# A feed-forward output by seven block products instead of eight, in three passes

## The chip, the cores and the metric

The kernel runs on one core of a Trainium2 chip. Its engines work beside each other, each through its own list of instructions in order: PE multiplies matrices into PSUM, DVE and ACT do elementwise work, POOL helps now and then, and SP issues most of the DMAs. The metric is the device time of one execution in microseconds (us), the median of several runs.

## The reference

One denoising step of a two-layer network on 512 latent and 128 prompt tokens, model width 1024, everything in fp32. Layer 0 mixes latent attention and neighbourhood attention, layer 1 is grouped-query attention. Every sub-layer is modulated by (shift, scale, gate), which come from two conditions (latent and prompt) through `w_mod`; each layer ends in a SwiGLU feed-forward of width D_FF = 2816 = 22 blocks of 128:

```python
hp = modulate(rms_norm(xp, norm_ffn[l]), sh2_p, sc2_p)
hs = modulate(rms_norm(xs, norm_ffn[l]), sh2_s, sc2_s)
xp = xp + g2_p * swiglu(hp, w_ffn_in[l], w_ffn_out[l])
xs = xs + g2_s * swiglu(hs, w_ffn_in[l], w_ffn_out[l])
...
def swiglu(h, w_in, w_out):
    gate, up = jnp.split(h @ w_in, 2, axis=-1)
    return (jax.nn.silu(gate) * up) @ w_out
```

Outputs are the normed token streams and the caches' new rows.

## The kernel before

Activations stand feature-major: a tile is 128 features by T = 640 tokens, worked on in two halves of HT = 320 columns (half 0 is latent; half 1 is 192 latent and 128 prompt columns, which is why a gated residual on it takes two instructions). Every fp32 product is three fp32r matmuls, high x high, high x low and low x high (`mm3`, L181): each operand is split by an ACT copy (the high part) and a DVE subtraction (the low part).

Layer 1's attention ends in an output projection (`mixer_out`, L1036, name "oc"): eight columns of 24 matmuls per half, a residual and a sum of squares for each, then the norm of half 0 and, later, of half 1. From the normed activations `ModS` makes the operands of the feed-forward ("h11...") with their sums and differences.

The feed-forward's input (`ffn`, L1126) does three hidden blocks directly and 19 by seven products instead of eight (Strassen's method as Winograd arranged it, on a 2 x 2 arrangement of gate/up by inner halves and of token halves). The seven products are named by their activation operand: a, D, N, b, c, C, E here, `11`, `"D"`, `"N"`, `21`, `22`, `"C"`, `"E"` in the code. Their weight operands wX, wY, wZ, wW are made per block from two raw 128 x 1024 tiles (L1210 to 1228). `close` (L1197) does a block's last product E after the next block's a and D, then silu, multiplication and `hidden` (L1152), which splits the block (640 columns at once) and writes its two halves to DRAM ("sp") through SP; the last three blocks stay.

The output (L1252 to 1350) needs all 22 hidden blocks for each of the eight output columns. It runs in two passes, over 9 and over 13 blocks, since PSUM and SBUF don't hold all; the blocks are read back from DRAM ("hr", `again`) into the ring of activation tiles and a pool "hd".

The gate of the feed-forward, G2, needs its own products of `w_mod` with the conditions: eight tiles of 512 KB ("wm"), on each of which DVE makes two multiply-and-sum passes of 128 x 1024 ("junk", L1364) against 1 MB of broadcast conditions ("cb"). `mod_side` (L1354) spreads them by a plan over the feed-forward's blocks (call at L1632). Layer 0's attention output has a similar helper beside it already (`beside`).

The order on each engine is set when the kernel is built, by a scheduler that walks the program with costs of its own; buffers of tile pools ("w", "ws", "u", "raw", with their counts) limit how far weights are prepared ahead.

Of the kernel before, what the change touches and what calls it, by code (L numbers as in the profile page):

```python
# [11 lines left out]
F32 = mybir.dt.float32  # L12
# [33 lines left out]
FO_ORDER = list(range(FB - 3, FB)) + list(range(FB - 3))  # L46


@with_exitstack
def body(ctx, tc, xT, vecs, crow, wm0, wm0g1, wm0g, wm1, wA, wNV, wNA, wMK, wMV, wOA, wGQ, wGK, wGV, wOC,  # L50
         wFI, wFO, cckvT, ckrT, cnkT, cnv, cgkT, cgv, rpbp, tabM, tabK, tabG, maskN,
# [199 lines left out]
    class ModS:  # L251


        def __init__(self, name, x, gsl, ml, sh, pools):
            pool, keep_ = pools

            a = keep_.tile([P, 2 * D], F32, tag="cb", bufs=1, name=name + "32a")
            d = [pool.tile([P, 1024], F32, tag="wr", bufs=2, name=f"{name}32d{i}") for i in range(2)]
            room = [t[:, j * HT:j * HT + HT] for t, n in ((a, 6), (d[0], 3), (d[1], 3)) for j in range(n)]
            room += [tp.tile([P, HT], F32, tag="u", bufs=7, name=f"{name}32u{i}") for i in range(4)]  # L260
            self.left, self.right = room[:KT], room[KT:]
# [774 lines left out]
    def mixer_out(wsrc, os_, order, xin, ml, name, nxt, pre, beside=None):  # L1036
# [5 lines left out]
        if True:  # L1042
# [13 lines left out]
            held = []  # L1056
            for n in range(KT):
                un = wunit(n)
                if beside and n >= 1:
                    beside(n - 1)  # L1060
# [49 lines left out]

    def ffn_open(l):
# [4 lines left out]
        hd = [[fk.tile([P, T], F32R, name=f"hd{l}_{i}{c}") for c in "hl"] for i in range(1)]  # L1116
        fs = ExitStack()
        fp = fs.enter_context(tc.tile_pool(name=f"fp{l}", bufs=1, reuse_waits="tile"))
# [5 lines left out]
        return ph, fk, dr, hd, fs, fp, w, pre  # L1124

    def ffn(l, x, pend, hm, nxt, side, opened):  # L1126
        ph, fk, dr, hd, fs, fp, w0, _ = opened
        turn = [0]

        def split(src, name):  # L1130

            turn[0] += 1
            t = (wp, fp)[turn[0] % 2].tile([P, 2, 1024], F32R, tag="w", bufs=3, name=name)
            S.activation(t[:, 0, :], src, AF.Copy)  # L1134
            V.tensor_tensor(t[:, 1, :], src, f(t[:, 0, :]), ALU.subtract)  # L1135
            return t[:, 0, :], t[:, 1, :]
# [13 lines left out]
        kept, spilt = {}, {}  # L1150

        def hidden(fb, sg):  # L1152

# [39 lines left out]
        hd += [[ring.tile([P, T], F32R, tag="hl", name=f"hd{l}_{i}{c}") for c in "hl"] for i in (1, 2)]  # L1193
# [14 lines left out]
        for fb in range(few, FB):  # L1208

            ru = load(wFI[l, fb, 1], 1024, f"wu{l}_{fb}r")  # L1210
            if fb == few:
                rg = load(wFI[l, fb, 0], 1024, f"wg{l}_{fb}r")
            else:
                rg = fp.tile([P, 1024], F32, tag="wr", bufs=2, name=f"wg{l}_{fb}r")
                nc.sync.dma_start(rg, wFI[l, fb, 0])
            wX = split(ru, f"wX{l}_{fb}")
            t = fp.tile([P, 2, 512], F32R, tag="w4", bufs=2, name=f"wW{l}_{fb}")
            wW = t[:, 0, :], t[:, 1, :]
            S.activation(wW[0], rg[:, 512:], AF.Copy)
            V.tensor_tensor(wW[1], rg[:, 512:], f(wW[0]), ALU.subtract)  # L1220
            s13 = fp.tile([P, 1024], F32, tag="ws", bufs=2, name=f"s13{l}_{fb}")
            V.tensor_tensor(s13[:, :512], rg[:, :512], rg[:, 512:], ALU.add)
            V.tensor_tensor(s13[:, 512:], ru[:, :512], rg[:, :512], ALU.add)
            wY = split(s13, f"wY{l}_{fb}")
            s24 = fp.tile([P, 1024], F32, tag="ws", bufs=2, name=f"s24{l}_{fb}")
            V.tensor_tensor(s24[:, :512], s13[:, 512:], rg[:, 512:], ALU.add)
            V.tensor_tensor(s24[:, 512:], s24[:, :512], ru[:, 512:], ALU.add)
            wZ = split(s24, f"wZ{l}_{fb}")
# [19 lines left out]
            job = fb, g, wW, up, sg  # L1248
        close(job)
# [541 lines left out]
```

## Time and profile before

| | us |
|---|---|
| median of 3 runs | 1519.8 |
| lowest and highest | 1515.85 and 1520.42 |
| the profiled execution's span | 1519.7 |

The span of the profiled execution is its time from first to last instruction; nothing of it is set apart, and its clock was 0.994 of full speed. In views by stage a row is a stretch of the span in us; in views by group a row is a line and engine, the operation, its tiles and shapes with the count, then busy time in us and the mean of one in ns, then idle time ahead of it and what ended it. In the chain of waits a row is a start, a duration, and what ran.

### The profile page before, as it was taken

What the parts mean: (1) busy time and instruction counts of PE and PEld (TensorE: products, weight loads), DVE (VectorE), ACT (ScalarE), POOL (GpSimd) and SP (SyncE); (2) the same over time, 40 slices, a digit from 0 to 9 for tenths busy, and PEclk for the clock granted to TensorE, in tenths of its full rate; (3) what the DMA queues carried; (4) which work ended last, traced back from release to release, by engine and by line L of the source; (5) the groups of instructions that cost most, each with busy time, mean ns of one, the idle gap of its engine ahead of it and who ended that gap; (6) DMA issues with size and microseconds to landing.
All of it is one profiled execution on the core that took longest, in us unless ns stands there. A gap on an engine that the chain in (4) does not pass through costs nothing. (4 is left out here: it accounts for less than half of the span.)

```text
span 1519.7 us, 25536 instructions
## 1 busy us (share of the span) xinstructions
PE 1467.1 (97%) x9894; PEld 1412.3 (93%) x9894; DVE 1134.0 (75%) x2150; ACT 737.9 (49%) x1426; POOL 176.7 (12%) x270
## 2 busy tenths in 40 slices
PE   5999999899999999999999999999999999999997
PEld 4989878889999999999999999989999999999997
DVE  5877788877878888946998888865988888833333
ACT  5446667753745555531223566653745555531221
POOL 0046636320000000000000122210000000000000
PEclk9999999999999999999999999999999999999999
DMA  9543341034164454568764200103154555466211
GB/s 373 197 150 119 119 136 43 15 111 153 46 219 145 163 166 162 182 210 321 234 228 133 91 29 29 56 15 97 47 205 154 170 167 167 133 245 232 86 42 70
DMA packets 73553, 215.08 MB, mean 142 GB/s; under 512 B 8152, under 2 KB 13048, under 8 KB 73048
## 3 DMA queue, kind: packets, MB, share of 16 engines
q1 hardware_dynamic: 71072, 209.04, 40.6%
q10 hardware_dynamic: 1944, 3.48, 0.7%
q8 instruction: 77, 1.26, 0.3%
q0 software_dynamic: 416, 0.93, 0.2%
q14 instruction: 44, 0.36, 0.1%
HBM read 184.96 MB, written 28.47 MB: 140 GB/s over the span
## 5 line engine op out<-in xcount | busy, mean ns | idle before, releaser
L1364 DVE SCALAR_TENSOR_TENSOR junk<-wm,cb 128x1024 bf16<-128x1024 f32 x104 | 126.8, 1220 | 3.6 <-DMA wm<-in_wm 2.9
L62 PE MATMUL gq<-h10h,wgq 128*128 128x320 f32 x256 | 65.8, 316 | 0.0
L246 POOL TENSOR_SCALAR h10h<-h10t,gs,mods 128x320 fp32r<-128x320 f32 x4 | 3.2, 792 | 439.1 <-DVE h10t L240 436.8
L1134 ACT ACTIVATE wY<-s 128x1024 fp32r<-128x1024 f32 x37 | 39.2, 1061 | 28.0 <-PE fg L62 22.5
L1134 ACT ACTIVATE wZ<-s 128x1024 fp32r<-128x1024 f32 x37 | 39.2, 1059 | 22.7 <-PE fd L62 20.7
L1135 DVE TENSOR_TENSOR wZ<-s,wZ 128x1024 fp32r<-128x1024 f32 x37 | 45.3, 1224 | 3.7 <-ACT wZ L1134 0.4
L1203 DVE TENSOR_TENSOR sg<-up,sg 128x640 f32<-128x640 f32 x37 | 30.4, 822 | 20.9 <-ACT sg L1202 20.7
L62 PEld LDWEIGHTS gq<-h10h,wgq 128*128 128x128 f32 x256 | 44.9, 189 | 0.6
L1135 DVE TENSOR_TENSOR wY<-s,wY 128x1024 fp32r<-128x1024 f32 x37 | 45.1, 1220 | 0.1
L62 PE MATMUL fg<-h01q,wgu 128*128 128x320 f32 x192 | 40.3, 316 | 0.9 <-ACT h01q L288 0.5
L1202 ACT ACTIVATE sg<-fg 128x320 f32<-128x320 f32 x37 | 16.2, 439 | 48.9 <-PE fg L62 48.9
L62 PE MATMUL gq<-h10l,wgq 128*128 128x320 f32 x128 | 39.5, 308 | 0.0
L1567 ACT ACTIVATE gp<-gs,gb,rq 128x640 f32<-128x640 f32 (+1 forms) x40 | 31.8, 795 | 15.3 <-DVE gb L1566 13.6
L314 DVE SCALAR_TENSOR_TENSOR xr<-fo,mods,xr 128x320 f32<-128x320 f32 (+2 forms) x48 | 19.6, 436 | 25.4 <-PE fo L62 25.3
L62 PE MATMUL fg<-h11N,wZ 128*128 128x320 f32 x228 | 36.6, 309 | 1.7 <-ACT p L1234 1.7
L1236 ACT ACTIVATE p<-fd 128x320 f32<-128x320 f32 x37 | 16.2, 438 | 45.2 <-PE fd L62 45.2
L62 PE MATMUL fg<-h11q,wX 128*128 128x320 f32 x228 | 36.7, 309 | 0.0
L62 PE MATMUL fg<-h11E,wW 128*128 128x320 f32 x228 | 36.6, 309 | 0.0
L62 PE MATMUL fd<-h11q,wZ 128*128 128x320 f32 x228 | 36.6, 309 | 0.0
L62 PE MATMUL fu<-h11q,wX 128*128 128x320 f32 x228 | 36.5, 309 | 0.0
L62 PE MATMUL fd<-h11D,wY 128*128 128x320 f32 x228 | 36.4, 308 | 0.0
L62 PE MATMUL fg<-h11C,wY 128*128 128x320 f32 x228 | 36.4, 308 | 0.0
(3055 smaller groups left out, 5299.1 us busy)
## 6 DMA issues: line engine op xcount, KB each, us to landing
wm<-in_wm SPq DMA_DIRECT2D x48, 512.0 KB, 4.3
mraw<-in_wm SPq DMA_DIRECT2D x8, 1024.0 KB, 13.1
mraw<-in_wm SPq DMA_DIRECT2D x16, 512.0 KB, 3.7
wmv<-in_wm0g SPq DMA_DIRECT2D x8, 512.0 KB, 3.6
wm<-in_wm0g SPq DMA_DIRECT2D x8, 512.0 KB, 5.3
x<-in_xT SPq DMA_DIRECT2D x8, 320.0 KB, 5.3
xr<-in_xT SPq DMA_DIRECT2D x8, 320.0 KB, 6.2
cb<-crs SPq DMA_DIRECT2D x2, 1024.0 KB, 7.8
```

What stands on the lines that cost most here:

```text
L62: cls.last = nc.tensor.matmul(*a, **k)
L246: G.tensor_scalar(h[:, c0:c1], t, self.gsl[:, k, 0:1], self.ml[:, self.sh + k, 0:1], ALU.mult, ALU.add)
L314: V.scalar_tensor_tensor(xo[:, c0:c1], ps[:, c0 - o:c1 - o], ml[:, g + n, c:c + 1], xi[:, c0:c1], ALU.mult, ALU.add)
L1134: S.activation(t[:, 0, :], src, AF.Copy)
L1135: V.tensor_tensor(t[:, 1, :], src, f(t[:, 0, :]), ALU.subtract)
L1202: last = S.activation(sg[:, 0:HT], g[:, :HT], AF.Silu, scale=-1.0)
L1203: V.tensor_tensor(sg, up, sg, ALU.mult)
L1236: S.activation(p5, b5[:, :HT], AF.Copy)
L1364: V.scalar_tensor_tensor(junk, raw, 1.0, cb[:, c, :], ALU.mult, ALU.mult, accum_out=mods[l][:, j0 + i, c:c + 1])
L1567: S.activation(dst, src, AF.Exp, bias=nb, scale=rq[:, j:j + 1], accum_out=ll[:, j:j + 1])
```

## The change

Layer 1's output product is done by the same seven-product scheme. The 22 hidden blocks are put in 11 pairs; a pair (inner halves) by two token halves is the 2 x 2 activation side, outputs n and n + 4 by the pair's blocks the weight side. `ffn_out_seven` runs three passes (`PASSES`): three pairs, then four, then four. A pass has four `Block`s (n = 0 to 3), each with seven products over the pass's pairs, three matmuls a pair: p1 uses a, p5 D, p6 N, p2 b, p3 c, p7 C, p4 E. p4 of a block stands after the next block's p1 and p5. Results go into the residual stream with the gate or, for the n + 4 outputs, the negated gate `ng`.

The operands' sums (D, N, C, E) are made in the input stage, in `hidden_pair`: after an even block two operands of 320 columns, after an odd one five, each by an ACT copy and a DVE subtraction, with four sums a pair. Nine pairs are spilled, seven tiles each (63 of 320 KB, where there were 38); pairs 9 and 10 stay. Pass 0 reads pair 8 back, the other passes 28 tiles each.

The weight preparation moves into a shared helper `seven`; layer 1's raw input weights use one "wr" buffer instead of two, and every other gate tile comes through the common raw buffers. Layer 1's G2 modulation (8 tiles, 16 passes of DVE, the conditions' load) moves from the feed-forward to the attention's output projection, by the numbers (2, 1, 1, 2, 1, 1, 0) of tiles at each column, and `early` has the column's own weights asked for first. The output weights are laid out anew (`wFO1`). Layer 0 keeps its method.

```diff
+PASSES = ((9, 8, 10), (0, 1, 2, 3), (4, 5, 6, 7))
+FO_PAIRS = [2 * p + i for ps in PASSES for i in range(2) for p in ps]
...
-    def mixer_out(wsrc, os_, order, xin, ml, name, nxt, pre, beside=None):
+    def mixer_out(wsrc, os_, order, xin, ml, name, nxt, pre, beside=None, early=False):
...
+                    if early:
+                        un(0)
...
+    def ffn_out_seven(x, nxt, opened, ops, spilt, split, close, last):
+
+        ph, fk, dr, hd, fs, fp, *_ = opened
+        ng = gs[0][0]
+        V.tensor_scalar_mul(ng, mods[1][:, G2:G2 + 8, :], -1.0)
...
+        def product(ps, wt, w0, pairs, what, first):
+            for k, p in enumerate(pairs):
+                a, b = [w[:, w0 + k * P:w0 + k * P + P] for w in wt]
+                t = ops[p, what]
+                mm3(ps[:, :HT], a, b, t[:, 0:HT], t[:, HT:T], first and k == 0, k == len(pairs) - 1, skip_group_check=not first)
...
+        def result(n, c, src, sign, end):
+
+            o = HALF[c][0]
+            for c0, c1, i in HCOND[c]:
+                V.scalar_tensor_tensor(x[n][:, c0:c1], src[:, c0 - o:c1 - o],
+                                       ng[:, n, i:i + 1] if sign < 0 else mods[1][:, G2 + n, i:i + 1], x[n][:, c0:c1], ALU.mult, ALU.add)
+            if end:
+                nrm.add(x[n], c)
...
+            def p1(self):
+                self.g = bank(f"fg{self.name}")
+                self.go(self.g, self.wX, 0, "a", True)
+                self.copy("p1", self.g)
+
+            def p5(self, kind="m", copied=True):
+                self.b5 = bank(f"fd{self.name}", kind)
+                self.go(self.b5, self.wY, 0, "D", True)
+                if copied:
+                    self.copy("p5", self.b5)
+
+            def p6(self):
+                self.go(self.g, self.wZ, 0, "N", False)
+                self.copy("u2", self.g)
+
+            def p2(self):
+                b2 = bank(f"fu{self.name}", "y")
+                self.go(b2, self.wX, 1, "b", True)
+                result(self.n, 0, self.add("p1", b2), 1, self.end)
+
+            def p3(self):
+                self.go(self.b5, self.wZ, 1, "c", False)
+                result(self.n, 1, self.add("u2", self.b5), 1, self.end)
+
+            def p7(self, ready=True):
+                self.go(self.g, self.wY, 1, "C", False)
+                if ready:
+                    result(self.n + 4, 1, self.add("p5", self.g), -1, self.end)
+                else:
+                    self.copy("u3", self.g)
+
+            def p4(self):
+                self.go(self.g, self.wW, 0, "E", False)
+                result(self.n + 4, 0, self.g, -1, self.end)
...
+        def again(p, what, pool, tag, bufs):
+            t = ops[p, what] = pool.tile([P, T], F32R, tag=tag, name=f"or{p}{what}", **({"bufs": bufs} if bufs else {}))
+            nc.sync.dma_start(f(t), spilt[p, what])
+
+        for what in PRODUCTS:
+            again(8, what, ring, "hh" if what in "aDNbc" else "hl", None)
+        b0 = Block(0, 0, 0)
+        b0.p1()
+        close()
...
+        for i, pairs in enumerate(PASSES):
+            if i:
+                for what in PRODUCTS:
+                    for p in pairs:
+                        if what in "aDNb":
+                            again(p, what, fo, "hd", 16)
+                        else:
+                            again(p, what, ring, "hl" if what == "E" else "hh", None)
...
+                if prev:
+                    prev.p4()
+                b.p6()
+                b.p2()
+                b.p3()
+                b.p7()
+                prev = b
...
+        e0, e1 = ends
+        e0.p1()
+        e0.p2()
+        prev.p4()
+        e1.p1()
+        e0.p6()
+        e1.p2()
+        e0.p7(False)
+        e1.p6()
+        e0.p4()
+        e1.p7(False)
+        e1.p4()
+        for b in ends:
+            b.p5(copied=False)
+            result(b.n + 4, 1, b.add("u3", b.b5), -1, True)
+            result(b.n, 1, b.held["u2"], 1, False)
+            if b is e0:
+                nrm.rstd(0)
+        for b in ends:
+            b.go(b.b5, b.wZ, 1, "c", False)
...
+        def operand_of(p, what, src):
+            t = ops[p, what] = pair_tile(p, what)
+            S.activation(t[:, 0:HT], src, AF.Copy)
+            V.tensor_tensor(t[:, HT:T], src, f(t[:, 0:HT]), ALU.subtract)
+            if p not in RESIDENT:
+                d = spilt[p, what] = dr.tile([P, T], F32, name=f"sp{p}{what}")
+                nc.sync.dma_start(d, f(t))
+
+        def hidden_pair(fb, sg):
+
+            p, odd = divmod(fb, 2)
+            le, ri = sg[:, 0:HT], sg[:, HT:T]
+            if not odd:
+                even[p] = sg
+                operand_of(p, "a", le)
+                V.tensor_tensor(le, le, ri, ALU.subtract)
+                operand_of(p, "D", le)
+                return
+            d, b12 = [even[p][:, c0:c1] for c0, c1 in HALF]
+            n, c = [utile(f"{q}{l}_{fb}") for q in "nc"]
+            V.scalar_tensor_tensor(n, ri, -1.0, d, ALU.mult, ALU.subtract)
+            operand_of(p, "N", n)
+            operand_of(p, "b", le)
+            operand_of(p, "c", ri)
+            V.tensor_tensor(c, ri, b12, ALU.subtract)
+            operand_of(p, "C", c)
+            V.scalar_tensor_tensor(n, n, -1.0, le, ALU.mult, ALU.subtract)
+            operand_of(p, "E", n)
...
+        if l:
+            return ffn_out_seven(x, nxt, opened, ops, spilt, split, lambda: close(job), lambda: last)
...
+    _, before = mod_side([(1, wm1[G2:], G2)], None)
+    x, pend = mixer_out(wOC, oGs, list(range(8)), lambda n, x=x: x[n], mods[1], "oc", nxt, op[-1],
+                        before(op[5], op[5], (2, 1, 1, 2, 1, 1, 0)), True)
...
-    side, _ = mod_side([(1, wm1[G2:], G2)], lambda kind, i: int(kind == "n" or i > 5 and i % 2 == 0))
-    x, pend = ffn(1, x, pend, box["m"], final, side, op)
+    x, pend = ffn(1, x, pend, box["m"], final, lambda pool: lambda kind, i: None, op)
```

On DVE, at the end of the attention's output projection ("oc" are its sums and weights, "xr" the residual stream, "wgu" the first feed-forward weights, "h11t" the first normed tile), there stood before:

```order
L172 TENSOR_TENSOR ocw_12359<-ocw7r,ocw_12359 128x1024
L206 TENSOR_TENSOR ocnacc<-ocnacc,ocnsq_12282 128x320
L314 SCALAR_TENSOR_TENSOR xr_4646<-oc5a,mods_99,xr_4646 128x320
L206 TENSOR_TENSOR ocnacc<-ocnacc,ocnsq_12317 128x320
L314 SCALAR_TENSOR_TENSOR xr_4684<-oc6a,mods_99,xr_4684 128x320
L206 TENSOR_TENSOR ocnacc<-ocnacc,ocnsq_12352 128x320
L314 SCALAR_TENSOR_TENSOR xr_4722<-oc_12355,mods_99,xr_4722 128x320
L206 TENSOR_TENSOR ocnacc<-ocnacc,ocnsq_12387 128x320
L282 TENSOR_TENSOR h11t_12461<-xr_4367,ocnrs 128x320
```

and now:

```order
L1602 SCALAR_TENSOR_TENSOR junk_12333,mods_99<-wm_46_12329,cbo 128x1024
L174 TENSOR_TENSOR ocw_12367<-ocw6r,ocw_12367 128x1024
L311 SCALAR_TENSOR_TENSOR xr_4646<-oc5a,mods_99,xr_4646 128x320
L1602 SCALAR_TENSOR_TENSOR junk_12372,mods_99<-wm_47_12370,cbo 128x1024
L208 TENSOR_TENSOR ocnacc<-ocnacc,ocnsq_12362 128x320
L1602 SCALAR_TENSOR_TENSOR junk_12374,mods_99<-wm_47_12370,cbo 128x1024
L174 TENSOR_TENSOR ocw_12409<-ocw7r,ocw_12409 128x1024
L1606 TENSOR_TENSOR mods_99<-mods_99,vec 128x16
L311 SCALAR_TENSOR_TENSOR xr_4684<-oc6a,mods_99,xr_4684 128x320
L174 TENSOR_TENSOR wgu_0_12444<-wgu_0r,wgu_0_12444 128x1024
L208 TENSOR_TENSOR ocnacc<-ocnacc,ocnsq_12404 128x320
L1176 TENSOR_SCALAR gs_100<-mods_99 128x16
```

Modulation passes ("junk") now stand between the residuals and ahead of the last weights' splits, and the feed-forward's first weights come after the last of these.

On DVE, in the input stage around odd block 13's multiplication ("sg"; "up" and "g" are sums that read PSUM, "s" weight sums, "w" splits), before:

```order
L1364 SCALAR_TENSOR_TENSOR junk_14942,mods_99<-wm_45_14940,cb 128x1024
L1226 TENSOR_TENSOR s_16_14749<-s_16_14743,wg_16r 128x512
L1364 SCALAR_TENSOR_TENSOR junk_14944,mods_99<-wm_45_14940,cb 128x1024
L1203 TENSOR_TENSOR sg_13_14357<-up_13_14356,sg_13_14357 128x640
L1220 TENSOR_TENSOR wW_15_14604<-wg_15r,wW_15_14604 128x512
L1227 TENSOR_TENSOR s_16_14749<-s_16_14749,wu_16r 128x512
L1156 TENSOR_TENSOR hd_1l<-sg_13_14357,hd_1h 128x640
L1242 TENSOR_TENSOR up_14_14492<-fu_14_14491,p_14_14494 128x320
L1135 TENSOR_TENSOR wX_16_14737<-wu_16r,wX_16_14737 128x1024
```

and now:

```order
L1451 TENSOR_TENSOR sg_13_14562<-up_13_14561,sg_13_14562 128x640
L1161 TENSOR_TENSOR wW_15_14832<-wg_15r,wW_15_14832 128x512
L1387 SCALAR_TENSOR_TENSOR n_13_14742<-sg_13_14562,sg_12_14408 128x320
L1391 TENSOR_TENSOR c_13_14743<-sg_13_14562,sg_12_14408 128x320
L1370 TENSOR_TENSOR op6N<-n_13_14742,op6N 128x320
L1370 TENSOR_TENSOR op6b<-sg_13_14562,op6b 128x320
L1370 TENSOR_TENSOR op6c<-sg_13_14562,op6c 128x320
L1370 TENSOR_TENSOR op6C<-c_13_14743,op6C 128x320
L1393 SCALAR_TENSOR_TENSOR n_13_14742<-n_13_14742,sg_13_14562 128x320
L1478 TENSOR_TENSOR up_14_14696<-fu_14_14695,p_14_14698 128x320
L1480 TENSOR_TENSOR up_14_14696<-fd_14_14694,u_14_14700 128x320
```

One split of 640 columns and a modulation pass went; three sums and five splits of 320 came, the last of them behind the next block's first two sums.

On SP, at the end of the second pass ("sp" is the spilled tile, "or" its place, "ru" and "rg" raw weights of a block), what stood from the middle of the output stage on before:

```order
L1275 DMA wo_0_60r<-in_wFO 128x640
L1275 DMA wo_0_65r<-in_wFO 128x512
L1256 DMA hr_18h<-sp_18h 128x640
L1256 DMA hr_18l<-sp_18l 128x640
L1275 DMA wo_0_75r<-in_wFO 128x512
L1275 DMA wo_1_01r<-in_wFO 128x768
L1275 DMA wo_1_11r<-in_wFO 128x768
L1275 DMA wo_0_70r<-in_wFO 128x640
```

and now, between the second and third pass:

```order
L1183 DMA rgo_1_17003<-in_wFO 128x1024
L1183 DMA ruo_2_17137<-in_wFO 128x1024
L1265 DMA or4a<-sp4a 128x640
L1265 DMA or5a<-sp5a 128x640
L1265 DMA or6a<-sp6a 128x640
L1265 DMA or7a<-sp7a 128x640
L1265 DMA or4D<-sp4D 128x640
L1265 DMA or5D<-sp5D 128x640
L1265 DMA or6D<-sp6D 128x640
L1265 DMA or7D<-sp7D 128x640
```

Reloads were spread among weight loads; now 24 of them (up to `or7C`) stand in one row behind the third block's first weights.

171 lines of the change are left out of this document (128 added, 43 removed).

## The prediction

> **What bounds the kernel now.** I read the page first, then the busy time by stage, then the chain of waits through the last feed-forward layer.
>
> ```profile
> span 1519.7 us, 25536 instructions
> PE 1467.1 (97%) x9894; PEld 1412.3 (93%) x9894; DVE 1134.0 (75%) x2150; ACT 737.9 (49%) x1426; POOL 176.7 (12%) x270
> ```
>
> ```profile
> 1026.80:1064.00 37.20, 37.20 (x254) 37.04 (x253) 19.42 (x36) 13.78 (x22) 2.41 (x1) 1.00 0.31 100
> 1200.00:1340.00 140.00, 140.00 (x957) 140.00 (x956) 118.09 (x166) 73.16 (x113) 0.00 (x0) 1.00 0.46 149
> 1356.00:1510.00 154.00, 153.00 (x1043) 152.58 (x1041) 55.20 (x97) 31.11 (x47) 0.00 (x0) 1.00 0.38 127
> ```
>
> Each row of the second fence is a stretch: its length, then busy time of PE, weight loads, DVE, ACT and POOL, the granted clock, the DMA share and GB/s. The first stretch is the output projection of layer 1's attention, the second its feed-forward input by seven products, the third its feed-forward output. In the last two PE never waits and the clock is full. In the output stage DVE is free two thirds of the time; in the input stage it has 21.9 us of 140 left.
>
> How fast PE issues is read from the chain, since a matmul's own duration overlaps its neighbours'.
>
> ```profile
> 1351.78 0.73 PE fo_0a L62 x5
> ...
> 1428.41 11.43 PE fo L62 x78
> ...
> 1509.02 0.02 issue
> ```
>
> 78 matmuls in 11.43 us are 0.1465 us each. The output stage before has 22 hidden blocks x 8 columns x 2 halves x 3 = 1056 of them: 154.7 us, which agrees with 1351.78 to 1509.02. One block of seven products (84 matmuls) takes 12.31 us, and a product over four pairs 1.76.
>
> **The gain.** After, the stage has 11 pairs x 4 blocks x 7 products x 3 = 924 matmuls. The 132 that go are worth 132 x 0.1465 = **19.3 us**, all on the path as long as PE stays the last to be waited for. Everything else in the change is work for DVE, ACT and the DMAs, costing only where it makes PE wait.
>
> **DVE in the input stage.** Durations of one, and idle time before it:
>
> ```profile
> L1135 DVE TENSOR_TENSOR wZ<-s,wZ 128x1024 fp32r<-128x1024 f32 x11 | 13.5, 1226 | 1.5
> L1364 DVE SCALAR_TENSOR_TENSOR junk<-wm,cb 128x1024 bf16<-128x1024 f32 x10 | 12.2, 1219 | 0.1
> L1203 DVE TENSOR_TENSOR sg<-up,sg 128x640 f32<-128x640 f32 x11 | 9.1, 823 | 4.4 <-ACT sg L1202 4.3
> L1242 DVE TENSOR_TENSOR up<-fu,p 128x320 f32<-128x320 f32 x12 | 5.9, 491 | 3.5 <-PE fu L62 3.5
> L1156 DVE TENSOR_TENSOR hd_1l<-sg,hd_1h 128x640 fp32r<-128x640 f32 x4 | 3.3, 824 | 0.6 <-ACT hd_1h L1155 0.6
> L1222 DVE TENSOR_TENSOR s<-wg_13r 128x512 f32<-128x512 f32 x1 | 0.7, 693 | 0.8 <-DMA wg_13r<-in_wFI 0.8
> L1281 DVE TENSOR_TENSOR wo_0a<-wo_0ar,wo_0a 128x768 fp32r<-128x768 f32 x1 | 1.0, 959 | 0.4 <-ACT wo_0a L1280 0.4
> ```
>
> ```profile
> L206 DVE TENSOR_TENSOR fn1acc<-fn1acc,fn1sq 128x320 f32<-128x320 f32 x13 | 6.4, 489 | 4.4 <-ACT fn1sq L205 4.4
> L314 DVE SCALAR_TENSOR_TENSOR xr<-fo,mods,xr 128x320 f32<-128x320 f32 x8 | 4.4, 550 | 8.0 <-PE fo L62 8.0
> L314 DVE SCALAR_TENSOR_TENSOR xr<-fo,mods,xr 128x192 f32<-128x192 f32 x8 | 3.3, 418 | 12.0 <-PE fo L62 12.0
> L314 DVE SCALAR_TENSOR_TENSOR xr<-fo,mods,xr 128x128 f32<-128x128 f32 x8 | 2.7, 342 | 0.0
> ```
>
> Before, a block has three splits of 1024 (3 x 1.226), five passes of 512 (5 x 0.69), three sums of 320 (3 x 0.49), the multiply and the split of 640 (0.82 each), and ten modulation passes are spread over the 11.4 blocks: 11.4 us by means. The stretch holds 140/12.31 = 11.4 blocks and 118.09 us busy, so 10.4 a block: consecutive operations overlap, and sums of means are to be taken times 0.91. After, without modulation and the 640 split, the common part is 9.4 by means; an even block adds three operations of 320 (two operands, one sum), an odd one eight (five operands, three sums). That is 10.9 and 13.3 by means, **9.9 and 12.1 us** in fact, 22.0 of the 24.6 that PE needs for the pair. DVE gets tight, but weight splits are made about a block ahead, so an odd block's lateness is made up in the even one. I cost it at nothing: PE's own 24.6 us cover it. ACT gains 7 x 0.44 - 2 x 0.74 = 1.6 us a pair, by these rows, on 6.4 a block (73.16 over 11.4); it has room.
>
> ```profile
> L1236 ACT ACTIVATE p<-fd 128x320 f32<-128x320 f32 x11 | 4.8, 438 | 14.5 <-PE fd L62 14.5
> L1155 ACT ACTIVATE hd_1h<-sg 128x640 fp32r<-128x640 f32 x4 | 3.0, 740 | 1.8 <-DVE sg L1203 1.8
> ```
>
> **DVE in the three passes.** One block of four pairs has the same splits (3 x 1.226 + 5 x 0.69), three sums and six gated additions (2 x 0.55, and 2 x (0.42 + 0.34 for the other 128 columns)): 11.2 by means, 10.2 us of PE's 12.31. With three pairs, splits of 768 and sums of 384, 8.8 of 9.23. In the last pass four squares' sums of 0.49 come on top: 12.0 of 12.31. So the first and last passes leave 0.4 and 0.3 us a block. If DVE also waits 1 us a block, each pass falls behind by 2 to 3 us, which the block prepared ahead should mostly take up. Bounds 0 and 5; I take **+1.0**.
>
> **The reloads.** Between the second and third pass 24 tiles of 320 KB (28 less E's four, loaded early) must come in, each into a place that the running block releases product by product.
>
> ```profile
> 1354.00:1364.00 10.00, 10.00 (x70) 10.00 (x69) 3.24 (x4) 4.16 (x5) 0.00 (x0) 1.00 1.04 400
> 1364.00:1374.00 10.00, 10.00 (x70) 10.00 (x69) 3.76 (x7) 1.48 (x2) 0.00 (x0) 1.00 1.04 395
> 1103.00:1117.50 14.50, 14.35 (x98) 14.09 (x97) 11.03 (x15) 5.42 (x8) 0.00 (x0) 1.00 0.81 286
> ```
>
> ```profile
> wo_70r<-in_wFO SPq DMA_DIRECT2D x1, 320.0 KB, 2.8
> ```
>
> The first two rows are such reloads, all engines busy: 395 GB/s, 0.83 us a tile. A lone tile lands in 2.8, 2.0 beyond that. Counting from the first matmul of the second pass's last block, its "a" tiles are free at 1.76, so tile number k lands at 1.76 + 0.83k + 2.0. PE comes to the new "a" at 12.3, D 14.1, N 17.6, b 19.3, c 21.1, and to C from 23.3 to 26.2, since the order mixes it with the next block's "a". The tightest is c's fourth tile: it lands at 20.4 and is needed at 22.4. The margin is 2.0 us. At the third row's 286 GB/s (1.15 a tile, a mixed stretch with engines only 0.81 busy) c's last would be 4.3 late and C's last another 0.8: 5.1 us. Bounds 0 and 5; the stretch is most like the first rows, so **+0.5**. The page "DMA: Bandwidth & Descriptors" of the Trainium skill, section "Where 436 GB/s comes from", says that HBM transfers are bound at about 358 GB/s per core; by that, an estimate, a tile takes 0.92 us and c's fourth lands at 22.1, 0.3 us ahead of its use, so the sum would stay but any slip of the queue would show. The two rows of 400 and 395 run above that figure, and the measurement decides.
>
> **The moved modulation.** Sixteen passes of 1.22 (and 0.08 to read each sum) go beside the attention's output projection.
>
> ```profile
> DVE xr L314 <- PE oc0a L62: 8.8, 1, 8.8
> ```
>
> ```profile
> 1052.67 3.52 PE oc6a L62 x24
> ...
> 1075.54 0.54 ACT ocnrs L213
> ...
> 1084.12 0.40 DVE h11t L282
> ...
> 1095.64 0.74 DVE hd_0l L1156
> ...
> 1103.97 6.82 DMA wg_3r<-in_wFI
> ...
> 1122.85 2.02 PE fg L62 x12
> ```
>
> DVE idles 8.8 us ahead of its first residual at 1026.8, and three passes stand there in the order. The other 13 (16.9 us) fall to 1026.8 to 1064, where DVE is now busy 19.42 of 37.2: 36.3 after, almost full, in an engine that also waits. PE has other columns' matmuls to go on with, but the first half's norm comes later, and from 1075.54 on the chain runs through ACT and DVE, so that lateness is handed on. At best 0, at worst one half column, 3.52; I take **+1.5**.
>
> **The transition to seven products.** The chain now waits 6.82 us for a weight load queued on SP behind the 1 MB conditions, which go. In its place stand 14 operations of 320 instead of three splits of 640 (14 x 0.40 - 3 x 0.74 = +3.4 us at the chain's spacing) on the DVE that the chain runs through.
>
> ```profile
> PE fg L62 <- ACT p L1234: 1.7, 1, 1.7
> ```
>
> PE's only long wait there is 1.7. Bounds -1.7 and +3.4: **+0.5**.
>
> **The rest.** The last hidden block must be split before the first pass can use it; PE has D, a and D (3 x 1.32 = 4.0 us) to do meanwhile, against a chain of silu, product, difference and split of about as much: bounds 0 and 4, and **+0.5**, as its pair stands last in each product. At the end four residual halves instead of two, and two output rows more, stand in DVE's order ahead of the last norm sum:
>
> ```profile
> 1509.04 0.69 DVE xr L314 x2
> ...
> 1510.25 0.50 DVE fn1acc L206
> ...
> 1512.77 0.55 DVE xr L1629
> ```
>
> one of those operations is on the path, 0.5 (bounds 0 and 1.1): **+0.5**. The 25 more spills (63 for 38) have 49 us of four blocks for 14 tiles, at 149 GB/s now: nothing, the DMA engines are 0.46 busy. The halved weight buffer, the negated gates and layer 0's shared helper: nothing, they are off PE's path.
>
> **Sum.** -19.3 + 1.5 + 0.5 + 0.5 + 1.0 + 0.5 + 0.5 = -14.8. The profiled execution has a span of 1519.7 us, 0.1 under the runs' median of 1519.8, and I set no time apart outside it. 1519.8 - 14.8 = **1505 us**.
>
> **Rivals.**
> *DVE becomes the bound (slower).* DVE now idles 1.93 us a block in the input stage (21.9 over 11.4). If that were latency, not running ahead, and every block kept it, a pair would take 25.9 against 24.6 (+1.2, times 9.5 pairs, 11.8), the first pass 10.7 against 9.23 (+6.0 over four blocks), the last 13.9 against 12.31 (+6.5): 24.3 us, **1529**. It decides from 1.77 us a block (20 us) for slower; below 1.3 the input stage is untouched. For it: the idle is spread over many waits, and DVE works in order.
>
> ```profile
> DVE wX L1135 <- ACT wX L1134: 6.4, 11, 0.6
> DVE sg L1203 <- ACT sg L1202: 4.3, 3, 3.4
> DVE up L1242 <- PE fu L62: 3.5, 6, 0.6
> ```
>
> Against it: waits on PE's "fu" are DVE running ahead, 3.4 of "sg" is a single start, and a split of ACT waits 7.7 us for a place that PE frees:
>
> ```profile
> L1134 ACT ACTIVATE wZ<-s 128x1024 fp32r<-128x1024 f32 x11 | 11.7, 1061 | 7.7 <-PE fd L62 7.7
> ```
>
> Such waits shrink when DVE is late. I give it 0.18.
>
> *The reload stalls PE.* 286 GB/s instead of 395: 5.1 us less 0.5 already in, **1510**; 0.13. For it: SP issues in order, and a weight load that waits for DVE stands directly ahead of the 24. Against it: that load's place is freed blocks earlier.
>
> *The early part costs more.* The attention stage at +3.5 and the transition at +3.4 are 4.9 more: **1510**; 0.11. Against it: the 8.8 us idle.
>
> *The change does not do what it says.* If the 924 matmuls ran at another spacing than the 1056, no gain; the shapes are the same, 128x128 by 128x320: 0.02.
>
> **Chances.** The forecast, 1500 to 1510 by its own bounds, has 0.56; the rivals have 0.18, 0.13, 0.11 and 0.02. A measurement of this kernel tells about 0.3% (4.6 us) from no change, so faster is under 1515.2 and slower over 1524.4. Of the first rival's 0.18 I put 0.03 below that band, 0.04 in it and 0.11 above. The two at 1510 could come together, 0.03, which makes 1515, the same. Faster: 0.56 + 0.13 + 0.11 - 0.03 + 0.03 = 0.80; same: 0.03 + 0.04 + 0.02 = 0.09; slower 0.11. The range of **1499 to 1519** takes in the forecast, the two at 1510, alone or together, and the first rival's milder part.
>
> **What would show it.** Right: PE busy throughout from the first seven-product block to the last residual, 924 matmuls between, a span of the output stage near 136 to 138 us; the attention stage's first norm 1 to 2 us later; no PE wait for an "or" tile at the third pass. Wrong: PE waiting for weight splits ("wX", "wY", "wZ") in odd blocks or the first and last pass, DVE without a gap there; PE waiting on DMA at "or4c" to "or7C"; or a norm of the attention stage over 3.5 us late.

## The result, and the profile after

The changed kernel takes 1504.2 us (median of 4 runs, 1499.56 to 1505.78) against 1518.94 of the kernel before (4 runs): a ratio of 0.9893, 95% interval 0.9872 to 0.9915. Taken again twice beside the experiments it gave 1502.11 against 1519.38 (0.9888, 0.9868 to 0.9907) and 1502.31 against 1519.24 (0.9891, 0.9878 to 0.9905). The forecast was 1505.

The first lines of its page:

```profile
span 1503.8 us, 25821 instructions
PE 1449.1 (96%) x9762; PEld 1392.3 (93%) x9762; DVE 1234.7 (82%) x2378; ACT 784.8 (52%) x1535; POOL 175.5 (12%) x270
```

132 matmuls fewer (9762 for 9894) and 18 us less PE time (1449.1 for 1467.1); DVE has 100.7 us more to do and ACT 46.9 more.

By stage: the input stage and the three passes of the output stage (the columns are those of the same view before):

```profile
1200.00:1340.00 140.00, 140.00 (x957) 140.00 (x957) 125.03 (x202) 82.12 (x144) 0.00 (x0) 1.00 0.51 165
1353.60:1389.70 36.10, 36.10 (x249) 36.08 (x248) 33.75 (x65) 20.70 (x35) 0.00 (x0) 1.00 0.84 295
1389.70:1438.00 48.30, 48.30 (x332) 48.30 (x331) 44.13 (x75) 20.05 (x28) 0.00 (x0) 1.00 0.64 220
1438.00:1484.50 46.50, 46.50 (x318) 46.23 (x317) 33.86 (x63) 19.60 (x34) 0.00 (x0) 1.00 0.36 138
```

PE does not pause in any of them, that is, up to the last twenty microseconds. DVE fills 125.03 of 140 us in the input stage, where the prediction had worked out 22.0 of 24.6 a pair, which is 125.1 of 140. From 1000 us on the longest waits of PE (what for, the sum in us, how often, the longest) are therefore few; "fn1p" and "ocnp" are the matmuls of the norms' sums, "gs" the attention's scores ahead of the stages in question:

```profile
PE fn1p L64 <- DVE fn1acc L208: 3.1, 2, 2.5
PE gs L64 <- ACT gp L1805: 1.6, 3, 0.7
PE ocnp L64 <- DVE ocnacc L208: 1.0, 2, 0.6
```

The 1.7 us of "PE fg <- ACT p" before are gone, and no "wX", "wY", "wZ" or "or" tile is among them.

To see where each microsecond went, I count from the first weight load of the product "oc0b" in the attention's output projection of layer 1. Up to it the engines have the same order of instructions in both kernels, yet this point comes at 1012.9 to 1018.6 us in one execution or another (much of it goes with the granted clock, which ahead of this point stood at half for 3.4 us in the earliest execution, fill's, and for 13.7 us in the latest, the changed kernel's first; part is one weight load of layer 0, whose wait in the chain was 8.76 us in one execution of the changed kernel and 7.03 in another). Counted from there, in us, with three of the experiments beside the two kernels:

| | before | before_moved | after | no_mod | dve2 |
|---|---|---|---|---|---|
| first normed tile (h11t) | 47.3 | 48.9 | 49.1 | 47.3 | 49.1 |
| first product N of the input stage | 106.1 | 106.5 | 106.5 | 104.5 | 106.5 |
| last product N of the input stage | 329.5 | 329.9 | 329.4 | 327.5 | 341.8 |
| last product c of the output stage ends | 492.3 | 492.7 | 473.8 | 471.8 | 485.4 |
| end | 502.9 | 503.9 | 485.3 | 482.9 | 496.4 |

The change gains 17.7 us from that point on: up to the input stage's last N nothing, in the output stage 18.4 (162.8 to 144.4), and the tail gives 0.8 back (10.7 to 11.5). The three pairs of medians say 14.7, 17.3 and 16.9.

How the modulation that was moved delays the norm is seen in the chain (start, duration, what ran):

```profile
1056.00 1.14 DVE junk L1602 x2
...
1057.54 1.15 DVE junk L1602 x2
1058.69 0.50 DVE ocw L174
...
1060.37 3.35 DVE wgu L174
1063.72 0.40 DVE ocnacc L208
...
1065.80 0.82 PE ocnp L64 x2
```

Where before the chain ran through PE ("oc6a", 24 matmuls), it now runs through DVE: two passes, then the split of the last weights "ocw", then a split "wgu" of 3.35 us, ahead of the first half's norm ("ocnp").

The end of the chain:

```profile
1474.91 7.03 PE fgo L64 x48
1481.94 0.59 PE fdo L64 x4
...
1485.74 0.50 DVE fn1acc L208
1486.29 0.81 PE fn1p L64 x2
1487.09 5.31 PE fdo L64 x36
...
1493.50 0.92 DVE xr L1869 x2
1494.42 0.41 DVE fn1acc L208
1494.88 1.30 PE fn1p L64 x2
```

The first half's norm matmul "fn1p" stands ahead of the last 36 "fdo" in PE's list, and its sum "fn1acc" is not ready in time. What that costs is read from PE's busy time between these two rows (length, then PE's busy time and count):

```profile
1481.94:1492.40 10.46, 9.88 (x62) 1.00 0.13 47
```

62 matmuls are 60 of products, 8.79 us at 0.1465 (x48 in 7.03 again), and the norm's two, 0.54 in the chain of the kernel before: 9.33. So PE loses 1.1 us. After the last product two output rows (L1869, 0.92) stand in DVE's list ahead of the last "fn1acc".

### The profile page after: what moved, and what is told of

It is laid out like the page before. It is cut to its first block, busy times and chain, and to the rows that moved or that the text cites. A ratio compares the mean times of both kernels' runs of the same rounds, so it can differ in the third digit from the quotient of the medians.

```text
span 1503.8 us, 25821 instructions
## 1 busy us (share of the span) xinstructions
PE 1449.1 (96%) x9762; PEld 1392.3 (93%) x9762; DVE 1234.7 (82%) x2378; ACT 784.8 (52%) x1535; POOL 175.5 (12%) x270
## 3 DMA queue, kind: packets, MB, share of 16 engines
q1 hardware_dynamic: 77152, 225.43, 44.9%
## 4 chain that ended last, share of the span: by engine, by line
PE 76%; DVE 10%; DMA 6%; ACT 5%; issue 2%; POOL 1%; SPq 0%; ACTq 0%; DVEq 0%; POOLq 0%
PE fg L64 19%; PE fd L64 8%; PE fgo L64 5%; PE fu L64 4%; PE gq L64 3%; PE fdo L64 2%; DVE junk L1602 2%; PE fo L64 2%; PE nk L64 2%; PE go L64 2%; PE gs L64 2%; PE nq L64 2%; DMA wm<-in_wm 1%; PE fuo L64 1%; DMA mraw<-in_wm 1%
## 5 line engine op out<-in xcount | busy, mean ns | idle before, releaser
L1602 DVE SCALAR_TENSOR_TENSOR junk<-wm,cb 128x1024 bf16<-128x1024 f32 x88 | 107.3, 1219 | 3.9 <-DMA wm<-in_wm 3.3
L1342 ACT ACTIVATE wY<-s 128x1024 fp32r<-128x1024 f32 x37 | 39.2, 1060 | 27.7 <-PE fg L64 24.0
L64 PEld LDWEIGHTS gq<-h10h,wgq 128*128 128x128 f32 x256 | 44.9, 189 | 0.6
L64 PE MATMUL fg<-h01E,wW 128*128 128x320 f32 x216 | 34.7, 310 | 0.4 <-DVE g L1482 0.4
```

The lines of the kernel that those rows point to most:

```text
L64: cls.last = nc.tensor.matmul(*a, **k)
L1342: S.activation(h, src, AF.Copy)
L1602: V.scalar_tensor_tensor(junk, raw, 1.0, cb[:, c, :], ALU.mult, ALU.mult, accum_out=mods[l][:, j0 + i, c:c + 1])
```

## The experiments

### The modulation: left out, and moved alone

*no_mod* is the changed kernel without layer 1's modulation of the gate and its loads: the gate is the bias alone.

```diff
+            if l and j0 == G2:
+                if i == 7:
+                    V.tensor_copy(mods[l][:, j0:j0 + 8, :], bc2(bmod(l, j0, 8)))
+                return
...
```

*before_moved* is the kernel before with nothing changed but the modulation's place:

```diff
...
-    x, pend = mixer_out(wOC, oGs, list(range(8)), lambda n, x=x: x[n], mods[1], "oc", nxt, op[-1])
+    _, before = mod_side([(1, wm1[G2:], G2)], None)
+    x, pend = mixer_out(wOC, oGs, list(range(8)), lambda n, x=x: x[n], mods[1], "oc", nxt, op[-1],
+                        before(op[1], op[5], (2, 1, 1, 2, 1, 1, 0)), True)
...
-    side, _ = mod_side([(1, wm1[G2:], G2)], lambda kind, i: int(kind == "n" or i > 5 and i % 2 == 0))
-    x, pend = ffn(1, x, pend, box["m"], final, side, op)
+    x, pend = ffn(1, x, pend, box["m"], final, lambda pool: lambda kind, i: None, op)
```

> The changed kernel without layer 1's G2 modulation: its 16 DVE passes, its tiles' loads and the conditions' load are left out, so the gate is only its bias. Theory 'handed on' (the prediction's +1.5): the attention stage's first norm comes 2 us earlier counted from the start of oc0b, and so does everything behind it; the whole is 1.5 to 2 us faster than the changed kernel, near 1502.5. Rival 'absorbed': the norm comes 2 us earlier too, but the seven-product blocks start at the same time within 0.5 us, because what ends last there is DVE's own work on operands and weights; the whole is within 0.5 us of the changed kernel, near 1504.

> The kernel before with only the modulation moved to the attention's output projection (same plan, weights asked for first); its output stays eight products in two passes. Theory 'handed on': +1.5 from the late norm, and at most -1.7 from the wait that goes with the 1 MB load: within 0.5 us of the kernel before. Rival 'absorbed': the late norm costs nothing by the first seven-product block, and the wait for wg_3r and PE's 1.7 us behind it go: 1.5 to 2.5 us faster than the kernel before.

Measured: no_mod 1500.87 us against 1520.25 (0.9867, 0.9842 to 0.9893). By the table, whose rows are rounded, its norm is 1.9 us ahead of the changed kernel's, and a lead of 1.9 to 2.0 stays through every row down to the last product; the end is 2.4 ahead. So the norm's lateness is handed on whole, and costs 1.9 us. before_moved took 1521.07 against the same 1520.25 (1.0006, 0.9993 to 1.0019): its norm is 1.7 us late, its first N only 0.4. The wait for "p", 1.7 us in the kernel before, is nearly gone:

```profile
PE fg L62 <- ACT p L1237: 0.3, 1, 0.3
```

and neither its chain nor the changed kernel's shows a load between 1060 and 1123 us, where the kernel before waited 6.82 us for "wg_3r". Moving the modulation costs 1.7 to 1.9 in one place and gives 1.3 to 1.6 back in the next. Whether it is the conditions' load or the passes that help by leaving, these runs don't separate.

### DVE made busier in the input stage

One (*dve1*) or two (*dve2*) more passes of 128 x 1024 in each of the 19 seven-product blocks, whose result nobody uses (the edit is that of *dve2*):

```diff
+            for i in range(2 * l):
+                junk = fp.tile([P, D], mybir.dt.bfloat16, tag="junk", bufs=1, name=f"extra{fb}_{i}")
+                V.scalar_tensor_tensor(junk, ru, 1.0, rg, ALU.mult, ALU.mult)
```

> The changed kernel with one more DVE pass of 128x1024 (1.14 us at the usual spacing) in each of layer 1's 19 seven-product input blocks. Theory of the prediction, that PE's time covers DVE as long as a pair stays under 24.6 us: 22.0 + 2.3 = 24.3 us a pair, so DVE near 99% busy there and 0 to 3 us slower than the changed kernel, at most 1507. Rival 'latency' (DVE's idle 1.3 us a block is waits that stay): each block is longer by what is added, 19 x 1.14 = 22 us, near 1526.

> The same with two more passes a block. Theory of the prediction: 22.0 + 4.6 = 26.6 us a pair against PE's 24.6, 2.0 x 9.5 = 19 us slower, near 1523, DVE without a gap. Rival 'latency': 43 us slower, near 1547. If neither, and the time is under 1512, DVE's share was overstated.

Measured: dve1 1501.71 us (two executions; 0.9876, 0.9837 to 0.9916), as the changed kernel; dve2 1513.53 (0.9953, 0.9938 to 0.9969), and by the table its end is 11.1 us later than the changed kernel's. 135 us of the input stage read, in the changed kernel and in dve1:

```profile
1200.00:1335.00 135.00, 135.00 (x923) 135.00 (x923) 120.17 (x191) 78.40 (x136) 0.00 (x0) 1.00 0.52 169
1200.00:1335.00 135.00, 135.00 (x923) 135.00 (x922) 130.91 (x207) 79.06 (x140) 0.00 (x0) 1.00 0.50 165
```

and the same of dve2:

```profile
1200.00:1335.00 135.00, 131.48 (x870) 127.24 (x869) 132.83 (x201) 71.53 (x127) 0.00 (x0) 1.00 0.45 169
```

and what PE waits for in dve2:

```profile
PE fg L64 <- DVE wZ L1343: 3.5, 5, 0.8
```

With DVE 97% busy instead of 89% PE does not miss one matmul (923 in both). Only when there is more DVE work than time does PE wait for split weights; the stage from first to last N becomes 235.3 us for 222.9. The idle time of DVE is thus a lead that shrinks, not a latency that each block keeps. The cost of dve2, 12.4 us, is less than the 19 expected: its 38 passes at the DVE's own spacing (1.14 in the chain) are 43.3 us, of which the idle time of the whole input stage (0.107 of some 223 us, 24) swallows most. The 7 us that are left I put down to DVE's lead at the stage's start, which no row shows by itself.

### The tail and the reloads

*after_again* is the changed kernel, unedited. *tail_a* holds four of the first half's eight outputs behind the last norm sum:

```diff
-        nxt(x, nrm, 0, range(KT), False)
+        nxt(x, nrm, 0, range(4), False)
...
+        def end():
+            nrm.rstd(1)
+            after(nrm.last, lambda: nxt(x, nrm, 0, range(4, KT), False))
+            nxt(x, nrm, 1, range(KT), False)
...
```

*tail_b* is tail_a with the first half's norm sums behind both last D products:

```diff
-            if b is e0:
-                nrm.rstd(0)
+        nrm.rstd(0)
```

*reload_more* puts eight more transfers of 320 KB, whose data nobody uses, on SP's queue ahead of the 24 reloads of the last pass:

```diff
+            if i == 2:
+                for k in range(8):
+                    t = dr.tile([P, T], F32, name=f"more{k}")
+                    nc.sync.dma_start(t, x[2])
```

> The changed kernel itself, unchanged, as the reference of this group: 0.989 of the kernel before, and from the start of oc0b to the end of the span 485 us.

> The changed kernel with the last four first-half outputs (L1869) held back in DVE's order until behind the last norm sum. In the changed kernel two of them (0.92 us) stand on the path between the last residual and that sum. Theory, that the tail is a chain through DVE: 0.9 us less from the last c product to the end (10.5 instead of 11.4). Rival, that they come back behind the norm: 0 to -0.3.

> tail_a, and the first half's norm sums (the fn1p matmuls) asked for behind both D products instead of between them. In the changed kernel PE waits there: 60 matmuls and the sums take 10.46 us where their spacing makes 9.33, so 1.1 us. Theory: that 1.1 goes too, 2.0 us less than the changed kernel from oc0b to the end, 483. Rival: the first half's outputs then come later and fill the tail, so no more than tail_a.

> The changed kernel with eight more transfers of 320 KB (stores of one residual tile to spare DRAM) issued directly ahead of the 24 reloads for the third pass. In the changed kernel the last c tile lands 0.9 us ahead of its use. Theory, that the row is bound by the DMA engines at 0.83 us a tile: 6.6 us more, some 2.8 of it in idle DMA time before the first place is free, so the row ends 3.9 us later and PE waits about 3 us (2 to 5) at the c and C products of the third pass's first block. Rival, that the row goes by the pace at which places come free: no wait of PE over 0.5 us, the same time as the changed kernel.

Measured against 1519.38: after_again 1502.11, tail_a 1501.2 (0.9882, 0.9864 to 0.9901), tail_b 1502.26 (0.9889, 0.9869 to 0.9909). Counted from the oc stage all three end at 484.8. Neither edit gains anything. In tail_b's chain PE's pause is gone ("fdo" runs on up to the norm matmul), but from 1486.30 to 1491.26 DVE has taken its place:

```profile
1481.72 2.94 PE fdo L64 x20
1484.66 0.55 PE fn1p L64 x2
...
1486.30 1.01 DVE xr L1873 x2
1487.32 0.40 DVE fn1acc L208
1487.72 0.59 DVE xr L1198 x2
1488.31 0.92 DVE xr L1873 x2
...
1491.30 1.28 PE fn1p L64 x2
```

Residuals, norm sums and outputs stand back to back on DVE. That one and the same program had a tail of 11.0 us in after_again, 11.5 in the first profile and 11.6 in after_third also says that the tail's 0.8 is hardly more than executions differ by.

reload_more took 1509.13 us (three executions: 1509.06, 1509.13 and 1512.95; 0.994, 0.992 to 0.996), 7.0 more than after_again, where 2 to 5 were expected. The profile is that of the longest of the three, and ends 10.4 us later than after_again's. On SP the reloads' row (first and last tile, then the next weights) reads, in the changed kernel:

```profile
1427.93 0.33 SPq L1265 DMA_DIRECT2D or4a<-sp4a  x1
...
1445.52 0.32 SPq L1265 DMA_DIRECT2D or7C<-sp7C  x1
1446.36 0.33 SPq L1183 DMA_DIRECT2D rgo<-in_wFO  x1
```

and in the experiment:

```profile
1425.02 6.28 SPq L1284 DMA_DIRECT2D more<-xr  x8
1431.39 0.70 SPq L1265 DMA_DIRECT2D or4a<-sp4a  x1
...
1449.99 0.32 SPq L1265 DMA_DIRECT2D or7C<-sp7C  x1
1450.81 0.33 SPq L1183 DMA_DIRECT2D rgo<-in_wFO  x1
```

Since the changed kernel's oc stage begins at 1018.6 and the experiment's at 1016.0, the weights "rgo" come 7.0 us later. The experiment's busy times from there on:

```profile
1424.00:1438.00 14.00, 13.89 (x95) 13.54 (x93) 11.90 (x21) 6.12 (x9) 0.00 (x0) 1.00 0.92 318
1438.00:1452.00 14.00, 13.84 (x92) 13.51 (x93) 3.89 (x8) 2.43 (x6) 0.00 (x0) 1.00 1.02 381
1452.00:1466.00 14.00, 12.98 (x86) 12.19 (x85) 8.96 (x19) 5.22 (x11) 0.00 (x0) 1.00 0.52 202
1466.00:1482.00 16.00, 12.72 (x82) 12.42 (x81) 15.74 (x29) 8.14 (x13) 0.00 (x0) 0.91 0.00 1
```

with one long wait of PE:

```profile
PE fgo L64 <- ACT p1o L1219: 3.3, 1, 3.3
```

A stretch of 14 us of the changed kernel's passes holds 98 matmuls. While the reloads run, in the first two rows, 3 and 6 are missing, 1.3 us; in the two rows after them 12 and some 28, 5.9 us. For the reloads themselves PE hardly waits (0.2 us, at "or6a"), not at the c and C products as the first theory had it; nor does the time stay the same, as by the second. DVE starves in the second row (3.89 us busy, 7.48 in the changed kernel), when the weights behind the reloads are late, has everything to do at once in the last (15.74 of 16), and PE waits for it. The changed kernel's row at the place of the second reads:

```profile
1440.20:1454.20 14.00, 14.00 (x98) 14.00 (x97) 7.48 (x14) 4.68 (x8) 0.00 (x0) 1.00 1.02 392
```

The remaining 3.2 of the 10.4 lie behind these rows, and some 2 us of that are the clock of this one execution. From 1479 to 1486 us the granted clock was 0.51, and 48 products of the chain took 9.90 us where the changed kernel's take 7.03:

```profile
1480.28 9.90 PE fgo L64 x48
```

These 2.9 us, part of which fall into the last of the four rows, are about what sets this execution apart from the other two (mean clock 0.991 against 0.996 and 0.994). The low clock begins while PE stands still for 3.3 us; whether that brought it on, this run does not show. So the slip of 7 us costs 7.0 by the medians, and what comes behind the reloads is the larger part of it: a late reload is dearer here by what is queued behind it than by itself.

In the changed kernel the margin was smaller than forecast. The table of transfers has for the tightest tile (size, time from issue to landing):

```profile
or7c<-sp7c SPq DMA_DIRECT2D x1, 320.0 KB, 6.6
```

Issued at 1442.21, it lands at 1448.8, and PE's first product with it starts at 1449.7: 0.9 us, where 2.0 had been worked out.

### Getting the modulation's 1.9 us back

Three orders of the same passes. *plan_last* moves one tile of the plan behind the last weights' split:

```diff
-                        before(op[5], op[5], (2, 1, 1, 2, 1, 1, 0)), True)
+                        before(op[5], op[5], (2, 1, 1, 2, 1, 0, 1)), True)
```

*fill* puts a fourth pass ahead of the first residual, where DVE waits 3.08 us for PE:

```diff
+                    if early and n == 1:
+                        fourth = lastpass[0]
...
-                                evac(i, c, ps[c])
+                                after(fourth if early and (i, c) == (0, 0) else None, lambda: evac(i, c, ps[c]))
```

*fill_plan* has both, and *after_third* is the changed kernel beside them.

> The changed kernel with the last two modulation tiles' places exchanged in their plan (one tile at the eighth column instead of the seventh), so that the split of the attention's last weights, ocw7, stands right behind the sixth residual and ahead of the last passes. Theory "ahead of the last split": the 1.8 us by which the attention's norm comes late (49.1 for 47.3 us after the stage's first weight load) stand ahead of that split, so the norm comes back to 47.3 to 47.8 and the end to 483.0 to 484 us after that point (485.2 in the changed kernel), 1 to 2 us faster. Theory "sum of DVE work": between 20 and 68 us DVE has as much to do in any order, so whatever the split gains is handed back by the passes behind it; the norm stays at 48.5 to 49.5 and the end at 484.5 to 485.5.

> The changed kernel with one more modulation pass (the fourth) ahead of the stage's first residual, in the 3.08 us for which DVE idles there. Theory "idle filled": a pass of 1.22 us leaves the full stretch behind it, so the first norm comes 1.2 us earlier, 47.9 us after the first weight load for 49.1, and the end at 484.0 for 485.2. Theory "not this stretch": the first norm's lateness arises only from the passes ahead of the last split, with slack between; norm and end stay within 0.3 us.

> Both edits together. If each is worth what its first theory says, the first norm stands at 47.3 us (it can't be earlier than with no modulation there) and the end at 482.9 to 483.3 us after the first weight load, about 2 us faster than the changed kernel; if neither is, 49.1 and 485.2.

> The changed kernel once more, beside the three before it on the same chip: first norm at 49.1 us and end at 484.7 to 485.2 us after the stage's first weight load.

| | us | ratio to 1519.24 | first norm | end |
|---|---|---|---|---|
| after_third | 1502.31 | 0.9891 (0.9878 to 0.9905) | 49.2 | 485.5 |
| plan_last | 1500.93 | 0.9878 (0.9863 to 0.9893) | 49.3 | 484.8 |
| fill | 1500.08 | 0.9881 (0.9865 to 0.9897) | 49.8 | 485.4 |
| fill_plan | 1503.41 | 0.9902 (0.9887 to 0.9916) | 49.7 | 485.2 |

None is faster than the changed kernel by more than the intervals allow. For fill neither theory holds: its norm came later, not 1.2 us earlier and not within 0.3. plan_last's numbers are those of "sum of DVE work", but the reason is not the one that I had written. Its last attention product ended 1.2 us earlier, 43.7 us after the stage's first load instead of 44.9; the last residual, which needs only that, still started at 45.7 (changed kernel: 45.6). DVE in plan_last, by the timeline (start, duration):

```profile
1055.77 1.22 DVE L1602 SCALAR_TENSOR_TENSOR junk<-wm,cbo 128x1024 bf16<-128x1024 f32 x1
...
1056.91 2.69 DVE L208 TENSOR_TENSOR ocnacc<-ocnacc,ocnsq 128x320 f32<-128x320 f32 x1
...
1059.81 0.54 DVE L311 SCALAR_TENSOR_TENSOR xr<-oc,mods,xr 128x320 f32<-128x320 f32 x1
1060.94 0.49 DVE L208 TENSOR_TENSOR ocnacc<-ocnacc,ocnsq 128x320 f32<-128x320 f32 x1 [0.59 <-ACT ocnsq L207]
```

and on POOL at the same time:

```profile
1055.79 3.47 POOL L174 TENSOR_TENSOR wgu<-wgu_1r,wgu 128x1024 fp32r<-128x1024 f32 x1 [50.74 <-ACT wgu L173]
```

An addition of 320 columns takes 2.69 us, and 0.49 the next time. It ends 0.34 us after POOL's split of "wgu_1" does (1059.60 and 1059.26). The changed kernel has the same meeting with another DVE instruction:

```profile
1060.29 3.43 DVE L174 TENSOR_TENSOR wgu<-wgu_0r,wgu 128x1024 fp32r<-128x1024 f32 x1
```

beside its POOL:

```profile
1060.23 2.40 POOL L174 TENSOR_TENSOR wgu<-wgu_1r,wgu 128x1024 fp32r<-128x1024 f32 x1 [50.76 <-ACT wgu L173]
```

and the kernel before does not have it: POOL's split began at 1047.95 there and DVE's was long over:

```profile
1042.07 1.23 DVE L172 TENSOR_TENSOR wgu<-wgu_0r,wgu 128x1024 fp32r<-128x1024 f32 x1 [1.86 <-ACT wgu L171]
```

So two things, one behind the other, hold the norm. In the changed kernel the late splits of "ocw6" and "ocw7" delay PE's last product of the first half by 1.9 us (44.9 for 43.0 before; the column ahead of it, "oc6a", already ends 1.1 late) and the meeting with POOL delays the residual behind it by 0.6 more; 0.75 come back because the norm's matmul no longer queues behind others on PE. In plan_last the first is down to 0.7 and the second up to 1.9. In fill and fill_plan the first half's norm is 0.5 to 0.7 later still; in fill a DVE instruction of 0.49 again takes 2.49 beside POOL, and the last residual starts 1.7 us behind its product (46.2 and 44.5). A version that also keeps POOL's split away from this place was not run; my estimate, by the residual's delay in plan_last, is up to 1.9 us.

## Why the prediction was right, point by point

- *The gain, -19.3.* The output stage went from 162.8 to 144.4 us, -18.4; its 924 products alone take 138.9 us from first to last, where 136 to 138 was named as the sign. The matmuls run at the spacing of before (7.03 us for 48). Most of the 0.9 that is missing is the 1.1 us that PE loses at "fn1p", which the prediction had nowhere. Taking that pause away (tail_b) gained nothing, since DVE then set the end.
- *DVE in the input stage, 0.* Right, with its working: 125.03 busy where 125.1 was forecast, and dve1 shows that even 97% costs nothing.
- *DVE in the three passes, +1.0; the opening of the first pass, +0.5; the reload, +0.5.* All three measured 0: no PE wait for a weight, for "or" tiles or for the last hidden block. The three rows have 111.7 us of DVE work, where the sizes by pass (8.8, 10.2 and 12.0 a block, four blocks each) make 124. The last pass, which the prediction had as nearly full, is the emptiest (33.86 of 46.50); the first two are full to 93% and 91%, since weights are prepared ahead: each pass uses 12 weight splits, and the three rows hold 10, 13 and 8.
- *The moved modulation, +1.5.* 1.9, by no_mod. The mechanism booked, a DVE almost full in front of the norm, is right; part of it is the meeting with POOL, which the prediction did not see.
- *The transition, +0.5.* This step of the prediction failed, and had the wrong sign: -1.5 to -2.0. The prediction put 14 operations on the DVE that the chain ran through; the chain there became PE's, and with the load of "wg_3r" no longer late nothing else took its place. before_moved shows that it belongs to the modulation's move, not to the new operands: the kernel before with that move alone gets the same 0.4 at the first N.
- *The tail, +0.5.* 0.8, and one program's executions differ by 0.6 there.

The sum booked -14.8 and the traces say -17.7, the medians -14.7 to -17.3. The difference of 2.9 is the transition (2.0 to 2.5) and the three costs that did not appear (2.0), less 0.9 of the gain, mostly the pause, 0.4 of the modulation and 0.3 of the tail. That the first pair of medians lies within 1 us of the forecast is therefore luck: the other two pairs are 2 us beyond it, and the terms miss in both directions. The mechanism, 132 matmuls fewer at the old spacing with PE the last to be waited for, is right. Of the rivals, "DVE becomes the bound" decided, by its own words, on whether DVE's idle time is latency; dve1 says that it is not, and dve2 that DVE does become the bound, by my estimate beyond about 27 more passes of 1.14 us (43.3 less the 12.4 that were paid; no run lies between 19 and 38). "The reload stalls PE" did not happen but was closer than its 0.13: the tightest tile landed 0.9 us ahead, and reload_more shows that a slip of 7 us there costs 7.0.

## What to carry to other kernels

Read the idle time of a helper engine as lead or as latency before pricing more work on it: the test is whether its waits are for a free buffer or an earlier product (they shrink when it is late), and one run that loads it to 97% settles it. When a load or a helper's work is moved out of a stage, price what it held up there as well as what it delays in its new place; here the two nearly cancelled. A margin on a queue is to be priced with what is queued behind it, and a gap that is closed on one engine in a tail or in front of a norm is worth only as much as the next engine's list allows.

## What the runs showed of the hardware

In these runs DVE and POOL did not work side by side on operations with two inputs in SBUF. In the changed kernel DVE's split, 1.23 us alone, took 3.43 when it began 0.06 after POOL's of 2.40, and ended 1.1 after it; in before_moved it took 3.31 beside the same 2.40. In dve1 and plan_last, where the two began within 0.04 us of each other, POOL's took 3.51 and 3.47, and DVE's next addition of 0.49 took 2.69. The durations are those of one waiting for the whole of the other. The Trainium skill, page "SBUF — State Buffer", section "SBUF: two separate sides", says that a DVE operation with two SBUF inputs and a GpSimd operation that reads SBUF take a shared pair of ports as an exclusive lock for the whole instruction; these rows agree.

The third pass's reloads ran at 396 GB/s between 1440 and 1446 us of the changed kernel, as fast as the rows from which the prediction took 395, but over the whole row, 1428 to 1448 us, the DMA moved 374. The row's first tile landed 4.2 us after its issue, at 1432.1, and c's fourth at 1448.8. In between the tiles landed 0.83 us apart, as had been taken, but for "or7D" and "or4N", which are 1.6 apart; so 19 tiles took 16.7 us instead of 15.8, which is most of the 1.1 us by which the margin is smaller. What passed in that gap the trace does not name. From issue to landing a tile took 6.6 to 7.3 us in the full row, against 2.8 alone.
